# S5 phase tables: computed in a preparation thread and kept in DRAM, or computed inside each S5 pair

## The chip, the cores and the metric

The kernel runs on one core of one Trainium2 chip. The metric is the device time of one execution in microseconds (us). The kernel before takes 1314.66 us (median of three runs: 1306.43, 1314.66 and 1315.25 us). "Faster" and "slower" are meant against that median.

## The reference

The reference is a trunk of four mixers, each followed by `x = layer_norm(ALPHA * x + mixer(x))`: gated linear attention (GLA), gated delta net (GDN), a state-space layer (S5), and GLA again. It is run twice: on one prompt of 512 tokens from a zero state, and on 8 samples of 8 tokens from given states. The model has 1024 channels; everything is float32, and all new states are outputs.

The S5 layer matters here. Its input projection gives `u` and a gate `z`, each 1024 wide. Its 64 groups have 16 channels and a complex diagonal state of 64 entries, with `h[t] = a * h[t-1] + B u[t]` and `y[t] = Re(C h[t]) + D u[t]`. Then come gelu, a gated linear unit with two 1024 x 1024 weights (`s5_glu`), the gate, and an output projection. The decay `a` is a magnitude times a phase. The kernel works on blocks of 8 tokens, so a prompt has 64 blocks, and it needs for every block index n the phase `a8^n` (cosine and sine) and the magnitude `r8`.

## The kernel before

**Tiling.** Channels lie on the 128 partitions, tokens along the free dimension (2 halves of 256 prompt and 32 sample tokens, 288 columns). Every dense projection is split into a rounded and a remainder part for activations and weights, and is written as three passes of `fp32r` matmuls with 288 moving columns. These are the matmuls `ps<-fx`. Weights come from DRAM through three raw buffers, and are split by ScalarE and VectorE into a ring of four slots. The matmuls of the recurrences themselves are float32 (`ps<-sb`).

**Order of the work.** The program is written as generator threads, each with a rank (a lower rank goes first), over the recording engine queues of the class `Core`. A planner, run when the program is built, keeps a model clock. Whenever an engine is free in that model, the ready operation of the lowest rank is put next on that engine's queue. On the chip each engine and the SP queue, which issues all DMAs, then works its queue strictly in that written order. All records pass through one helper, so every instruction bears line 408. The dense projections (rank 10) run through all layers as one stream; recurrence threads fill the queues beside them.

**Memory.** Scratch memory is one pool of 32,960 words per partition. A thread gets a piece only when the pool holds that piece and the words that its thread must leave free (`keep`), and otherwise waits for a free. The dense stream leaves `reserve` words (2500 during GDN). GDN pairs after the first leave 2000. S5 pair j leaves 3500 until all earlier pairs have signalled `h`:

```
            if sum(h[1] for h in self.holes) >= prod(shape) + keep():
                v = self.alloc(shape, dt, long)
...
                self.go(self.s5_pair(g, j), 3 + j, f's5_{j}',
                        lambda j=j: 0 if all(f'h{i}' in self.events for i in range(j)) else 3500)
```

**The S5 preparation** is the thread `s5_prep0` (line 1899, rank 3), which starts with the kernel and runs beside GLA and GDN. It computes the angles of 6 doublings (`lc`, `ls`, 6 x 32 words each) and the magnitude `r8` (32 words), then calls `s5_prep` four times (tables stored to DRAM as `s5G`, `s5C`, `s5K`), then `s5_phase` four times. One `s5_phase` (line 2037) takes a table `R` of 3 x 8 x 64 words and two scratch pieces of 256 words. GpSimd sets three columns, VectorE copies `r8` into a plane of 8 x 63, and six doublings of six VectorE operations each (over 8, 16, 32, 64, 128 and 256 elements) fill the cosine and sine planes. The table is then stored to DRAM (`s5R`, 768 KB). Last, eight transfers rearrange `s5K` into `s5Kx` (512 KB each), and `s5prep` is signalled.

**The S5 pairs** (`s5_pair`, line 2217, ranks 3 to 6). There are four, with 16 groups each. Pair j starts once the constants are there (`s5c`) and, for j > 1, once `u` of unit 2j-1 is stored. It loads half a table (`st <- s5G`) and its phase table (`R <- s5R`), and waits for `u` of units 2j and 2j+1. It allocates and loads `U` (1,152 words, eight transfers from `Ud`), allocates `E` (1,024 words) and `Es`, and multiplies. Then VectorE rotates by `R`, scans and rotates back. The starting states come into `H` by a transfer of 64 KB from `s5_h1`. Four VectorE operations complete `H`, and `h{j}` is signalled. Two products with `s5Kx` and `s5C`, a gelu, eight stores to `Yd` and one load give `yx{2j}` and `yx{2j+1}`, which the dense stream waits for, one after the other, in its first three `s5_glu` units (`fm_first`, 18 matmuls for each `yx`).

Of the kernel before, what the change touches and what calls it, by code (L numbers as in the profile page):

```python
# [19 lines left out]
P = 128  # L20
# [3 lines left out]
NS, LS = 8, 8  # L24
# [7 lines left out]
S5_G, S5_P, S5_C, S5_T, S5_N = 64, 64, 16, 8, 72  # L32
# [582 lines left out]
class Kernel(Core):  # L615
# [779 lines left out]
    def gdn_gates(self, g, pab):  # L1395

        yield from self.wait('gdnpre')
        R = (yield from self.A(640))[:40]
        self.gpsimd.memset(R, 0.0)
        t1, t2 = (yield from self.A(2, HW)), (yield from self.A(2, HW))  # L1400
# [18 lines left out]
        for src, p0 in ((u2, 0), (ab[32:40], 32)):  # L1419
            d = R[p0:p0 + 8]  # L1420
            self.cp(d[:, 0:512].rearrange("p (a n) -> p a n", a=2), src[:, :, 0:256])
            for i in range(2):
                self.cp(d[:, 512 + 64 * i:576 + 64 * i].rearrange("p (a n) -> p a n", a=2), src[:, :, 256:HW])
        self.free(pab, t1, t2)
        yield R
        self.sync.dma_start(out=g['gcd'], in_=R[0:8, 0:576])
        self.sig('gcd')
        pc = yield from self.bank()
        for c in range(5):
            self.tensor.transpose(pc[:, c * 40:c * 40 + 40], R[:, c * P:c * P + P], self.ident[:40, :40])  # L1430
        C = yield from self.A(5, 40)
# [467 lines left out]
    def s5_prep0(self):  # L1899
# [3 lines left out]
        s = self.s5v = {}  # L1903
        tmp = []

        def T(name, *shape):
            s[name] = t = yield from self.A(*(shape or (G,)), long=True)
            if not shape:
                tmp.append(t)
            return t  # L1910
# [18 lines left out]
        lc, ls, r8 = (yield from T('lc', 6, 32)), (yield from T('ls', 6, 32)), (yield from T('r8', 32))  # L1929
# [53 lines left out]
        self.Kx = self.dram('s5Kx', [P, S5_G, P])  # L1983
        self.Gd = self.dram('s5G', [8, P, 8, P])
        self.Cd = self.dram('s5C', [8, P, 8, P])
        self.Rd = self.dram('s5R', [4, P, 3, 8, 64])
        z = yield from self.A(8, P)
        self.gpsimd.memset(z, 0.0)
        yield z
# [4 lines left out]
        for j in range(4):  # L1994
            yield from self.s5_prep(j)
        self.free(*[s[n] for n in ('sgn', 'ar', 'ai', 'cre', 'cim', 'ars', 'ais', 'dT', 'delta')])
        for j in range(4):
            yield from self.s5_phase(j)
        self.free(s['lc'], s['ls'], s['r8'])
        for t in range(S5_T):  # L2000
            self.sync.dma_start(out=self.Kx[16 * t:16 * t + 16], in_=self.Kd[:, :, 16 + 16 * t:144 + 16 * t]
                                .rearrange("g c n -> c g n"))
# [34 lines left out]
    def s5_phase(self, j):  # L2037

        s, t2 = self.s5v, self.TT
        q = slice(8 * j, 8 * j + 8)  # L2040
        R = yield from self.A(3, 8, 64)
        m1, m2 = (yield from self.A(8, 32)), (yield from self.A(8, 32))
        self.gpsimd.memset(R[:, 0, :, 0:1], 1.0)
        self.gpsimd.memset(R[:, 1, :, 0:1], 0.0)
        self.gpsimd.memset(R[:, 2, :, 0:1], 0.0)
        self.vector.tensor_copy(out=R[:, 2, :, 1:], in_=s['r8'][:, q].unsqueeze(2).to_broadcast([P, 8, 63]))
        for k in range(6):
            n = 1 << k
            cb, sb = (v.unsqueeze(2).to_broadcast([P, 8, n]) for v in (s['lc'][:, k, q], s['ls'][:, k, q]))
            rc, rs = R[:, 0, :, 0:n], R[:, 1, :, 0:n]  # L2050
            a, b = m1[:, :, 0:n], m2[:, :, 0:n]
            t2(a, rc, cb, ALU.mult)
            t2(b, rs, sb, ALU.mult)
            t2(R[:, 0, :, n:2 * n], a, b, ALU.subtract)
            t2(a, rc, sb, ALU.mult)
            t2(b, rs, cb, ALU.mult)
            t2(R[:, 1, :, n:2 * n], a, b, ALU.add)
            yield R[:, 1]
        self.free(m1, m2)
        yield R  # L2060
        self.sync.dma_start(out=self.Rd[j], in_=R)
        self.free(R)

    def s5_prep(self, b):

# [106 lines left out]

    def s5_consts(self, g):
        yield from self.wait('s5prep')
        g['h2'] = self.load((yield from self.A(3, 32, NS, long=True)), 's5_h2')
        g['bg'] = self.load((yield from self.A(16, long=True)), 's5_bglu')
        g['hs'] = yield from self.A(2, 32, NS, long=True)
        g['hp'] = yield from self.A(S5_G, long=True)
        self.sig('s5c')
# [37 lines left out]
    def s5_pair(self, g, j):  # L2217

        N, NP = S5_N, S5_N - NS
        def maps(src):  # L2220
            st = yield from self.A(8, P)
            self.load(st, None, src)
            return st

        yield from self.wait('s5c', *([f'u{2 * j - 1}'] if j > 1 else []))
        st = yield from maps(self.Gd[2 * j])
        R = yield from self.A(3, 8, 64)
        self.load(R, None, self.Rd[j])
        yield from self.wait(f'u{2 * j}', f'u{2 * j + 1}')
        U = yield from self.A(16, N)  # L2230
        for s in range(S5_T):
            self.sync.dma_start(out=U[16 * s:16 * s + 16],
                                in_=g['Ud'][j][:, :, :, s].rearrange("m g c n -> c (m g) n"))
# [36 lines left out]
        self.TT(M2, E[:, ::-1], sb, ALU.mult)  # L2270

        H = yield from self.A(16, N + 1)
        self.load(H[:, :, 0:NS], None, self.a['s5_h1'][:, 16 * j:16 * j + 16])
        self.gpsimd.memset(H[:, :, NS:NS + 1], 0.0)
        yield [M1, M2]
        for ri in range(2):
# [8 lines left out]
        hs, t = g['hs'][:, :, q], (yield from self.A(2, 8, NS))  # L2285
# [28 lines left out]
        if j == 3:  # L2314
            yield [g['hs'], g['hp']]
            self.sync.dma_start(out=self.o['s5s'], in_=g['hs'])
            self.sync.dma_start(out=self.o['s5p'], in_=g['hp'])
            self.free(g['hs'], g['hp'], g['h2'])
        yield from self.wait('udead')
        yield yf  # L2320
        for e in range(2):
# [58 lines left out]
```

## Time and profile before

| | |
|---|---|
| runs | 1306.43, 1314.66, 1315.25 us |
| profiled execution | 1305.55 us, of which the span is 1303.7 us |
| instructions | 23,541 |
| busy | TensorE 96%, VectorE 74%, ScalarE 46%, GpSimd 13% |
| DMA | 198.35 MB moved, mean 152 GB/s |
| granted TensorE clock, mean | 0.986 of 2.4 GHz |

Rough stretches of the profile, in us from the span's start: first GLA to about 255, its output projection to 312, GDN to about 640, its output projection to 713, S5 input projections to 875, gated unit and output projection to about 1000, last GLA to the end. The preparation thread stores its phase tables between 277.5 and 386.8 us, and writes `s5Kx` from 386.1 to 406.5 us.

How to read it: a busy TensorE says little by itself, since ends of matmuls are modelled; the matmul count in a stretch and the granted clock say how fast it went. Waits name the work that ended last before an instruction could start. "SPq" is the queue that issues the DMAs.

### The profile page before, as it was taken

The page shows a single profiled execution, that of the slowest core. Times are in us where ns is not written, and L with a number is a line of the kernel's source. Part 1 is how long each engine was busy: PE and PEld are TensorE (multiplying, and loading weights), DVE is VectorE, ACT ScalarE, POOL GpSimd, SP SyncE. Part 2 cuts the span into 40 slices and gives each one's busy share as a digit, 9 for nine tenths or more (in the row PEclk, how much of TensorE's full clock was granted, in tenths as well). Part 3 has the DMA queues.
Part 4 walks back from the last instruction along what each step waited for, and adds up shares of the span by engine and source line. Part 5 has one row for each costly group of instructions (what it writes and reads, how often), then busy time and mean ns, then how long its engine had stood idle before and what let it go on. Part 6 is the DMA issues. An engine that isn't in the chain of part 4 may idle for free.

```text
span 1303.7 us, 23541 instructions
## 1 busy us (share of the span) xinstructions
PE 1255.2 (96%) x8795; PEld 1175.5 (90%) x8795; DVE 964.5 (74%) x2117; ACT 599.9 (46%) x1317; POOL 164.6 (13%) x303
## 2 busy tenths in 40 slices
PE   9999999999998899999999999999999999999997
PEld 8898998779998888999987999999998899999986
DVE  5989888999998989989679439544245877554557
ACT  5565454514966667555442334453232255343330
POOL 5510000011221311232002000000000200000001
PEclk9999999999998999999999989999999999999999
DMA  7335645734368727445364798862234423243242
GB/s 230 115 97 163 208 138 165 252 103 166 102 167 241 183 80 201 122 134 158 118 223 168 217 246 195 231 194 89 81 115 152 141 96 115 88 140 128 98 154 73
DMA packets 129537, 198.35 MB, mean 152 GB/s; under 512 B 47176, under 2 KB 85960, under 8 KB 127376
## 3 DMA queue, kind: packets, MB, share of 16 engines
q1 hardware_dynamic: 129424, 196.86, 49.8%
q8 instruction: 69, 1.13, 0.4%
q14 instruction: 44, 0.36, 0.1%
HBM read 153.64 MB, written 47.37 MB: 154 GB/s over the span
## 4 chain that ended last, share of the span: by engine, by line
PE 62%; DVE 22%; DMA 6%; ACT 4%; issue 4%; POOL 1%; SPq 1%; POOLq 0%; DVEq 0%; ACTq 0%
PE ps L408 62%; DVE sb L408 18%; DVE fx L408 4%; ACT sb L408 3%; DMA sb<-Ud 2%; POOL sb L408 1%; ACT L408 1%; ACT fx L408 1%; SPq L408 1%; DMA s5Kx<-s5K 1%; DMA sb<-in_gdn_s 0%; DMA sb<-scr 0%; DMA sb<-in_rst 0%; DMA sb<-s5Kx 0%; DMA sb<-in_gla_q 0%
## 5 line engine op out<-in xcount | busy, mean ns | idle before, releaser
L408 PE MATMUL ps<-fx 128*128 128x288 f32 (+2 forms) x6736 | 1045.0, 312 | 8.0 <-ACT sb L408 2.9
L408 PEld LDWEIGHTS ps<-fx 128*128 128x128 f32 x6736 | 947.8, 190 | 57.6 <-issue 6.5
L408 DVE TENSOR_TENSOR fx<-sb,fx 128x1024 fp32r<-128x1024 f32 (+5 forms) x308 | 252.8, 845 | 164.5 <-ACT fx L408 160.8
L408 ACT CAST fx<-sb 128x1024 fp32r<-128x1024 f32 (+5 forms) x312 | 221.1, 735 | 302.1 <-PE ps L408 257.4
L408 PE MATMUL ps<-sb 128*128 128x128 f32 (+10 forms) x2059 | 292.7, 292 | 32.3 <-DVE sb L408 17.7
L408 PEld LDWEIGHTS ps<-sb 128*128 128x128 f32 (+6 forms) x2059 | 244.3, 175 | 61.9 <-DVE sb L408 20.4
L408 DVE TENSOR_TENSOR sb<-sb 128x128 f32<-128x128 f32 (+26 forms) x667 | 263.9, 414 | 13.5 <-ACT sb L408 3.9
L408 ACT COPY sb<-ps 128x512 f32<-128x512 f32 (+10 forms) x233 | 91.8, 411 | 120.6 <-PE ps L408 66.0
L408 ACT ACTIVATE sb<-sb 128x128 f32<-128x128 f32 (+10 forms) x239 | 108.9, 504 | 72.7 <-DVE sb L408 63.6
L408 DVE SCALAR_TENSOR_TENSOR sb<-sb 128x512 f32<-128x512 f32 (+7 forms) x205 | 133.5, 660 | 10.2 <-POOL sb L408 7.4
L408 POOL TENSOR_TENSOR sb<-sb 128x1 f32<-128x1 f32 (+4 forms) x46 | 72.5, 1581 | 526.6 <-DVE sb L408 511.0
L408 DVE SCALAR_TENSOR_TENSOR sb<-sb,ps 128x256 f32<-128x256 f32 (+3 forms) x216 | 92.1, 457 | 38.1 <-PE ps L408 27.5
L408 ACT ACTIVATE sb<-ps 128x128 f32<-128x128 f32 (+2 forms) x176 | 66.9, 382 | 74.7 <-DVE sb L408 40.4
L408 DVE SCALAR_TENSOR_TENSOR sb<-ps,sb 128x128 f32<-128x128 f32 (+3 forms) x112 | 55.2, 502 | 31.8 <-PE ps L408 25.3
L408 DVE COPY sb<-ps 128x256 f32<-128x256 f32 (+8 forms) x99 | 37.8, 388 | 51.0 <-PE ps L408 32.5
L408 POOL COPY sb<-sb 128x24 f32<-128x24 f32 (+4 forms) x92 | 40.2, 460 | 237.6 <-DVE sb L408 138.5
L408 ACT CAST fx<-ps 128x512 fp32r<-128x512 f32 (+2 forms) x32 | 17.6, 550 | 74.5 <-PE ps L408 74.4
L408 ACT ACT_TABLE_LOAD x37 | 47.5, 1283 | 1.3 <-PEq L2369 0.7
L408 ACT ACTIVATE sb<-ps,sb 128x128 f32<-128x128 f32 (+2 forms) x93 | 37.9, 440 | 21.1 <-PE ps L408 18.4
L408 POOL MEMSET sb<- 128x3 f32 (+10 forms) x96 | 29.3, 328 | 125.7 <-DVE sb L408 55.9
L408 POOL CAST fx<-sb 128x32 fp32r<-128x32 f32 (+1 forms) x33 | 10.6, 351 | 227.2 <-PE ps L408 199.8
L408 ACT ACTIVATION_READ_ACCUMULATOR sb<-ps 128x1 f32 x136 | 27.2, 200 | 0.1
(25 smaller groups left out, 250.4 us busy)
## 6 DMA issues: line engine op xcount, KB each, us to landing
sb<-in_gla_v SPq DMA_DIRECT2D x16, 512.0 KB, 3.7
sb<-in_gla_r SPq DMA_DIRECT2D x16, 512.0 KB, 4.0
sb<-in_gla_s SPq DMA_DIRECT2D x8, 1024.0 KB, 6.2
out_s_gla<-sb SPq DMA_DIRECT2D x8, 1024.0 KB, 4.3
sb<-in_gla_out SPq DMA_DIRECT2D x16, 512.0 KB, 3.7
sb<-in_gdn_s SPq DMA_DIRECT2D x32, 256.0 KB, 3.4
sb<-in_s_glu SPq DMA_DIRECT2D x16, 512.0 KB, 4.3
xres<-sb SPq DMA_DIRECT2D x12, 512.0 KB, 3.2
```

What stands on the lines that cost most here:

```text
L408: fn(*args, **kw)
```

## The change

The phase table is no longer computed in the preparation thread and stored. Each S5 pair calls `s5_phase` in place of its load of `R`, and uses the table that it returns. The angles `lc`, `ls` and `r8` (416 words) are freed after the fourth call instead of at the end of the preparation. The starting states `s5_h1` are loaded once, whole (512 words, 256 KB), with the S5 constants, and each pair's `H` is filled by a GpSimd copy from them instead of by a transfer.

```
--- before.py
+++ after.py
@@ -1983,7 +1983,6 @@
         self.Kx = self.dram('s5Kx', [P, S5_G, P])
         self.Gd = self.dram('s5G', [8, P, 8, P])
         self.Cd = self.dram('s5C', [8, P, 8, P])
-        self.Rd = self.dram('s5R', [4, P, 3, 8, 64])
         z = yield from self.A(8, P)
         self.gpsimd.memset(z, 0.0)
         yield z
@@ -1994,9 +1993,6 @@
         for j in range(4):
             yield from self.s5_prep(j)
         self.free(*[s[n] for n in ('sgn', 'ar', 'ai', 'cre', 'cim', 'ars', 'ais', 'dT', 'delta')])
-        for j in range(4):
-            yield from self.s5_phase(j)
-        self.free(s['lc'], s['ls'], s['r8'])
         for t in range(S5_T):
             self.sync.dma_start(out=self.Kx[16 * t:16 * t + 16], in_=self.Kd[:, :, 16 + 16 * t:144 + 16 * t]
                                 .rearrange("g c n -> c g n"))
@@ -2057,9 +2053,10 @@
             t2(R[:, 1, :, n:2 * n], a, b, ALU.add)
             yield R[:, 1]
         self.free(m1, m2)
-        yield R
-        self.sync.dma_start(out=self.Rd[j], in_=R)
-        self.free(R)
+        s['phases'] = s.get('phases', 0) + 1
+        if s['phases'] == 4:
+            self.free(s['lc'], s['ls'], s['r8'])
+        return R
 
     def s5_prep(self, b):
 
@@ -2172,6 +2169,7 @@
 
     def s5_consts(self, g):
         yield from self.wait('s5prep')
+        g['h1'] = self.load((yield from self.A(S5_G, NS, long=True)), 's5_h1')
         g['h2'] = self.load((yield from self.A(3, 32, NS, long=True)), 's5_h2')
@@ -2224,8 +2222,7 @@
 
         yield from self.wait('s5c', *([f'u{2 * j - 1}'] if j > 1 else []))
         st = yield from maps(self.Gd[2 * j])
-        R = yield from self.A(3, 8, 64)
-        self.load(R, None, self.Rd[j])
+        R = yield from self.s5_phase(j)
         yield from self.wait(f'u{2 * j}', f'u{2 * j + 1}')
@@ -2270,7 +2267,7 @@
         H = yield from self.A(16, N + 1)
-        self.load(H[:, :, 0:NS], None, self.a['s5_h1'][:, 16 * j:16 * j + 16])
+        self.gpsimd.tensor_copy(out=H[:, :, 0:NS], in_=g['h1'][:, 16 * j:16 * j + 16])
         self.gpsimd.memset(H[:, :, NS:NS + 1], 0.0)
@@ -2315,7 +2312,7 @@
-            self.free(g['hs'], g['hp'], g['h2'])
+            self.free(g['hs'], g['hp'], g['h1'], g['h2'])
```

## Rows read from the trace of the kernel before

**Rows 1.** The page's part 1: busy us, share of the span, instructions.
```profile
PE 1255.2 (96%) x8795; PEld 1175.5 (90%) x8795; DVE 964.5 (74%) x2117; ACT 599.9 (46%) x1317; POOL 164.6 (13%) x303
```
**Rows 2.** Windows: length, busy us (instructions) of PE, PEld, DVE, ACT, POOL; clock, DMA share, GB/s.
```profile
350.00:390.00 40.00, 38.41 (x279) 37.51 (x279) 38.02 (x111) 29.78 (x74) 10.44 (x29) 1.00 0.57 154
...
710.00:730.00 20.00, 15.89 (x113) 14.55 (x113) 14.31 (x25) 5.09 (x8) 0.62 (x2) 1.00 0.82 303
730.00:750.00 20.00, 20.00 (x152) 20.00 (x151) 6.24 (x7) 7.49 (x9) 0.00 (x0) 1.00 0.67 166
```
**Rows 3.** Windows, as above, of two short disturbed stretches and one in GDN.
```profile
395.00:400.00 5.00, 2.84 (x22) 2.60 (x20) 4.93 (x13) 2.85 (x11) 0.21 (x1) 0.98 1.07 318
400.00:410.00 10.00, 7.85 (x25) 6.59 (x26) 8.27 (x31) 6.84 (x31) 0.32 (x1) 0.50 1.04 305
765.00:770.00 5.00, 3.12 (x21) 2.92 (x19) 1.23 (x1) 1.14 (x2) 0.00 (x0) 0.84 1.03 332
770.00:780.00 10.00, 10.00 (x50) 10.00 (x50) 5.16 (x12) 3.38 (x9) 0.00 (x0) 0.57 0.95 251
450.00:460.00 10.00, 6.96 (x38) 6.23 (x39) 8.96 (x27) 9.94 (x23) 0.66 (x2) 0.83 0.59 160
```
**Rows 4.** Timeline of DVE, the second phase table: start, us, instructions merged, count.
```profile
310.98 1.97 DVE L408 TENSOR_TENSOR sb<-sb 128x16 f32<-128x16 f32 x11
...
313.47 5.09 DVE L408 TENSOR_TENSOR sb<-sb 128x64 f32<-128x64 f32 x16
```
**Rows 5.** DVE groups by form, 257.5 to 386.5 us: busy us, mean ns, idle before.
```profile
L408 DVE TENSOR_TENSOR sb<-sb 128x16 f32<-128x16 f32 x24 | 3.6, 174 | 0.3
...
L408 DVE COPY sb<-sb 128x504 f32<-128x504 f32 x4 | 1.7, 416 | 1.6 <-DMA s5R<-sb 1.6
```
**Rows 6.** The chain of waits, 311 to 414 us: start, us, what.
```profile
318.59 3.37 DMA s5R<-sb
...
406.46 6.93 DMA s5Kx<-s5K
```
**Rows 7.** Timeline of PE: start, us, what, count, idle before and its releaser.
```profile
401.57 2.07 PE L408 MATMUL ps<-sb 128*128 128x256 f32 x4 [3.73 <-DVE sb L408]
...
768.08 6.79 PE L408 MATMUL ps<-sb 128*128 128x72 f32 x32 [1.88 <-issue]
...
836.87 19.71 PE L408 MATMUL ps<-fx 128*128 128x288 f32 x146
```
**Rows 8.** Timeline of the SP queue: start, us of issuing, transfer, count.
```profile
393.58 1.75 SPq L408 DMA_DIRECT2D sb<-in_gdn_q  x1
...
747.31 0.43 SPq L408 DMA_DIRECT2D sb<-s5R  x1
...
761.22 0.44 SPq L408 DMA_DIRECT2D sb<-Ud  x1
...
799.82 1.80 SPq L408 DMA_DIRECT2D sb<-Ud  x4
...
815.81 5.19 SPq L408 DMA_DIRECT2D Yd<-sb  x8
...
822.07 0.39 SPq L408 DMA_DIRECT2D sb<-s5G  x1
```
**Rows 9.** The page's part 6, DMA issues: count, KB each, median us to landing.
```profile
sb<-Ud SPq DMA_DIRECT2D x32, 72.0 KB, 6.3
```
**Rows 10.** Timeline of DVE and ACT at the end of the S5 pairs.
```profile
846.59 1.39 DVE L408 TENSOR_TENSOR sb<-sb 64x512 f32<-64x512 f32 x2 [1.40 <-DMA sb<-in_s_h]
...
882.64 2.72 DVE L408 TENSOR_TENSOR fx<-sb,fx 128x512 fp32r<-128x512 f32 x4
...
876.00 0.65 ACT L408 ACTIVATE sb<-ps 128x576 f32<-128x576 f32 x1
```
**Rows 11.** Timeline of POOL: two copies of one shape in GDN.
```profile
332.29 0.21 POOL L408 COPY sb<-sb 128x24 f32<-128x24 f32 x1
...
336.56 1.17 POOL L408 COPY sb<-sb 128x24 f32<-128x24 f32 x1
```

More of the change, by code (lines that the diff above doesn't have):

```diff
@@ L1985, in s5_prep0 @@
         self.Cd = self.dram('s5C', [8, P, 8, P])
-        self.Rd = self.dram('s5R', [4, P, 3, 8, 64])
         z = yield from self.A(8, P)
@@ L1996, in s5_prep0 @@
         self.free(*[s[n] for n in ('sgn', 'ar', 'ai', 'cre', 'cim', 'ars', 'ais', 'dT', 'delta')])
-        for j in range(4):
-            yield from self.s5_phase(j)
-        self.free(s['lc'], s['ls'], s['r8'])
         for t in range(S5_T):
@@ L2059, in s5_phase @@
         self.free(m1, m2)
-        yield R
-        self.sync.dma_start(out=self.Rd[j], in_=R)
-        self.free(R)
+        s['phases'] = s.get('phases', 0) + 1
+        if s['phases'] == 4:
+            self.free(s['lc'], s['ls'], s['r8'])
+        return R
     def s5_prep(self, b):
@@ L2174, in s5_consts @@
         yield from self.wait('s5prep')
+        g['h1'] = self.load((yield from self.A(S5_G, NS, long=True)), 's5_h1')
         g['h2'] = self.load((yield from self.A(3, 32, NS, long=True)), 's5_h2')
@@ L2226, in s5_pair @@
         st = yield from maps(self.Gd[2 * j])
-        R = yield from self.A(3, 8, 64)
-        self.load(R, None, self.Rd[j])
+        R = yield from self.s5_phase(j)
         yield from self.wait(f'u{2 * j}', f'u{2 * j + 1}')
@@ L2272, in s5_pair @@
         H = yield from self.A(16, N + 1)
-        self.load(H[:, :, 0:NS], None, self.a['s5_h1'][:, 16 * j:16 * j + 16])
+        self.gpsimd.tensor_copy(out=H[:, :, 0:NS], in_=g['h1'][:, 16 * j:16 * j + 16])
         self.gpsimd.memset(H[:, :, NS:NS + 1], 0.0)
@@ L2317, in s5_pair @@
             self.sync.dma_start(out=self.o['s5p'], in_=g['hp'])
-            self.free(g['hs'], g['hp'], g['h2'])
+            self.free(g['hs'], g['hp'], g['h1'], g['h2'])
         yield from self.wait('udead')
```

## The prediction

> **What bounds the kernel now.** I read the shares of busy time first [rows 1]: TensorE is busy 96% of the span, the next engine, VectorE, 74%. So at most some 48 us of TensorE's idle time can be won, plus what it loses where it is busy at a low clock. The windows come next, because that loss has places. In the stretch where the second half of the phase tables is computed, TensorE is idle 1.6 of 40 us while VectorE is busy 38.0 [rows 2]: VectorE is full there, but TensorE hardly waits for it. Two short places are much worse [rows 3]. From 395 to 410 us TensorE is idle 2.16 + 2.15 = 4.3 us, and for the last 10 us its granted clock is 0.50, the lower of its levels of 1.2 and 2.4 GHz; the 7.85 us in which it was busy there did half their work, 3.9 us lost. Together 8.2 us. From 765 to 780 us it is idle 1.88 us, and loses 3.12 x 0.16 + 10.00 x 0.43 = 4.8 us at granted clocks of 0.84 and 0.57. Together 6.7 us. In both places the DMA share is 0.95 to 1.07: all sixteen engines are in use. In both the low clock follows a wait of TensorE [rows 7].
>
> The queue and the chain say what filled the DMA engines. At the first place it is the eight `s5Kx` copies, which begin when the last phase table is done; one of them stands with 6.93 us in the chain of waits, and an earlier phase-table store with 3.37 us [rows 6]. A GDN weight is issued among them at 393.58 [rows 8], and TensorE stops soon after. At the second place the load of pair 2's table (768 KB, issued 747.31) goes ahead of most of pair 1's `U` transfers, the last of which is issued at 761.22 [rows 8]; with the usual 6.3 us to landing [rows 9] that gives 767.5, and TensorE's wait ends at 768.08 [rows 7]. The profile names no releaser there, so this is a reading.
>
> **The change part by part.**
>
> *The tables leave the preparation.* One table is 37 VectorE operations: 1.97 + 5.09 us for 27 of them [rows 4], one copy of 0.42 us and nine of the smallest at about 0.17 us [rows 5], together 9.0 us; four are 36 us. They go from a stretch where VectorE is full. What that frees goes to the GDN threads and to weight splits; on TensorE it is worth no more than its idle time there, 1.6 us, and I count it as nothing, with gains of up to 1.6 us. Four stores of 768 KB go too, with the GpSimd instructions that queue behind one.
>
> *The `s5Kx` copies move* ahead of where the tables were, from 386 to 406 us to right behind the last `s5_prep`, by about 285 us. The weights in flight there are those of GDN's first units, which run only from about 312 us, so I expect no new wait; they also no longer meet GDN's solve. That should take away most of the 8.2 us. But GDN's next hard stretch is short of memory rather than of DMA: from 450 to 460 us TensorE is idle 3.0 us [rows 3], and the dense stream, which must leave 2500 words, stands still there by the sizes of the code until GDN's pieces are freed. It now also lacks the 416 words of the angles. Between a full gain of 8.2 us and a loss as large as one more such stretch (3.0 us and 6.96 x 0.17 = 1.2 us at the low clock, 4.2 us) I take a gain of 6 us, nearer to the measured stall, since its cause is gone.
>
> *The tables enter the pairs.* Pairs 0 and 1 start both at about 710 us, while VectorE still finishes the layer norm; from 710 to 750 us it is idle 5.7 + 13.8 = 19.5 us [rows 2], which holds the 18 us of two tables, and their `U` is loaded only at 742 us and later. Layer-norm operations have lower ranks, but each may wait behind a table operation of up to 0.42 us: 1 us lost, between 0 and the 4.1 us that TensorE idles there today. Pair 2's table has the time from 747 us to its `u`. The load of its `R` is gone from the front of pair 1's `U` loads; of the 6.7 us I take 3, because the `U` transfers still share the engines with weights (bounds 0 and 6.7).
>
> *Pair 3 and memory.* This is where the change adds a wait. By the sizes of the code, pair 3 asks for `U` (1,152 words) with 3,500 to be left, 4,652 in all; when pair 1 signals `h1` it finds 4,944 and loads from 799.82 us [rows 8]. With 512 words of `s5_h1` more in use it finds 4,432, and must wait until pair 0 is done, whose `Yd` stores begin at 815.81 [rows 8]. `E` had to wait for that moment before, too, so the first product, then possible at about 816, now waits for eight issues of 0.45 and a landing of 6.3 us [rows 8, 9], and perhaps for the 5.2 us of the `Yd` issues ahead: 10 to 15 us. Part of that was lost anyway, since the second half's table was issued only at 822.07 [rows 8]: with 6 us of it back, 4 to 9 us. The 1.4 us that VectorE waited for `s5_h1` in pair 3 goes [rows 10]. Against this stands slack: the last `z` unit is done by 876.0, six `yx` parts of 18 matmuls at 19.71/146 = 0.135 us take 14.6 us more, so pair 3's result is needed by 890.6 at the latest, and its last write ends at 885.4 [rows 7, 10]: 5.2 us. 4 to 9 less 1.4 less 5.2 is a stall of 0 to 2.4 us; I take 2 us lost.
>
> *`s5_h1` in one transfer, copied by GpSimd.* Four transfers of 64 KB become one of 256 KB, early. The copies have 128 elements; the nearest rows are GpSimd copies of 24, which took 0.21 us, or 1.17 us while VectorE worked on two inputs [rows 11]. The place is beside two such VectorE operations, so up to 1.2 us each, under operations that `H` waits for anyway: nothing, bounds 0 and 1 us for each of four.
>
> The Trainium skill, "SBUF — State Buffer", section "Who interferes with whom", speaks against this step: a VectorE instruction with two inputs in SBUF and a GpSimd instruction that reads SBUF exclude one another, so that the later one waits for the whole of the earlier. The two copies bear it out (0.21 against 1.17 us). By the rule alone each new copy would cost an operation's length, some 5 us for four; by the rows it falls beside the same two operations.
>
> The sum is -6 + 1 - 3 + 2 = -6 us. The profiled execution (1305.55 us: the span of 1303.7 and 1.85 around it) would come to 1299.5. It lies 9.1 us under the median of the three runs, of which one is near it and two are near 1315; I put the same difference to the median: **1308 us**.
>
> **The rivals.**
>
> *Both bad places go whole, and the next ones too.* For it: each has one named transfer as its neighbour, and the change removes or moves exactly these. Against: 36 us of VectorE work remain. 8.2 + 6.7 + 1.6 = 16.5 us off: 1298 us.
>
> *The gain is given back.* TensorE is 96% busy, its queue order is written against a model, and GDN waits for memory in any case. If the dense stream, ahead by 6 us, stands still that much longer at 450 us, the first gain is gone; with S5's 3 us against 1 and 2 the time is 1314 us, up to 1322 with the extra stretch of 4.2 us and the upper bound of layer norm.
>
> *Slower: pair 3 late.* One mechanism: `U` refused for 220 words. It decides from the point where pair 3's last write falls after 890.6 us. With the whole 15 us and none back, TensorE stands 15 - 5.2 = 9.8 us, and such a wait is followed by a low clock, 4.8 us as measured at 765. With the other terms absent: 1314.7 + 14.6 = 1329 us. Against: six of the 15 us were lost before, too.
>
> *The tables are not hidden in the pairs.* If a pair's 9 us stood between its `u` and its `U`, pair 3 would end 9 us later. The code puts the table before the wait for `u`, and pair 3 begins when `u5` is stored, two units before `u7`: no separate case, but part of the slower one.
>
> **How the numbers follow.** I take about 1%, 13 us, for what a measurement of this kernel can tell from no change: its own runs lie 9 us apart. Chances: forecast 0.45 (1302 to 1313), both places whole 0.21, given back 0.21, pair 3 late 0.13. Faster by over 1% is under 1301.5: the second case and 0.03 of the first, 0.24. Slower by over 1% is above 1327.8: 0.12 of the last case and 0.01 of the third, 0.13. The rest, 0.63, is within 1%. The range 1291 to 1324 leaves out 0.06 below and the last case above.
>
> **What would show it.** Right: no `s5R` transfer; `s5Kx` issued before 300 us; granted clock 1.00 and no wait of several us near 400 us; `U` of pair 1 landed before TensorE comes to it, with no low clock near 770; `U` of pair 3 issued only after pair 0's `Yd` stores; TensorE going on without a wait through the first gated units. Wrong: a wait before the last `yx` parts with a low clock behind it, VectorE late at the layer norm (waits of TensorE near 715 us above 4.1 us), or a longer standstill of dense matmuls in GDN. The forecast falls first if the written order of GDN changes so far that new waits arise where none is now; no row can price that.

## The result and the profile after

The changed kernel takes **1318.72 us** (median of 10 runs, 1315.05 to 1323.52), the kernel before, on the same chip, 1311.05 us (median of 10, 1304.83 to 1315.25): a ratio of **1.0069**, 95% interval 1.0044 to 1.0093. That is a loss of some 8 us where a gain of 6 was forecast; it lies inside the range, and within the 1% that were taken for no change. The two profiled executions differ by 11.0 us: the span is 1314.7 us instead of 1303.7.

Part 1 of the page of the changed kernel, as in [rows 1]:

```profile
span 1314.7 us, 23536 instructions
...
PE 1253.8 (95%) x8795; PEld 1175.3 (89%) x8795; DVE 962.5 (73%) x2109; ACT 591.3 (45%) x1316; POOL 169.1 (13%) x307
```

VectorE, ScalarE and TensorE do nearly the same work; the 11 us are time in which TensorE stands or runs at its lower clock. To see where, I add up, over windows of 5 us, TensorE's idle time (length less busy) and what its clock cost (busy times 1 less the granted clock). The three stretches are GDN, the S5 pairs with the units around them, and the first gated units (us lost, of one profiled execution each):

| kernel | span | 340 to 700 | 700 to 860 | 860 to 920 |
|---|---|---|---|---|
| before | 1303.7 | 25.4 | 12.3 | 0.0 |
| after | 1314.7 | 24.2 | 13.3 | 11.1 |

The loss is at the end of the S5 pairs. In the kernel before, TensorE is busy without a break there (columns as in [rows 2]):

```profile
880.00:900.00 20.00, 20.00 (x152) 20.00 (x152) 11.88 (x16) 9.15 (x12) 0.00 (x0) 1.00 0.22 67
```

The windows there and at the places of [rows 2, 3], of the changed kernel (columns as there):

```profile
350.00:390.00 40.00, 34.78 (x239) 33.62 (x238) 30.62 (x73) 21.83 (x62) 7.31 (x24) 0.96 0.47 124
395.00:400.00 5.00, 5.00 (x40) 4.51 (x39) 4.94 (x13) 4.51 (x9) 1.24 (x3) 1.00 0.10 10
402.60:405.60 3.00, 0.03 (x2) 0.02 (x1) 2.97 (x9) 2.74 (x8) 0.00 (x0) 0.98 0.72 192
400.00:410.00 10.00, 6.21 (x28) 4.89 (x26) 9.69 (x36) 5.79 (x25) 0.00 (x0) 0.83 0.65 184
760.00:765.00 5.00, 5.00 (x26) 5.00 (x25) 1.76 (x10) 1.46 (x5) 0.00 (x0) 0.50 1.02 370
765.00:770.00 5.00, 5.00 (x31) 5.00 (x31) 4.44 (x21) 1.28 (x4) 0.00 (x0) 0.77 0.96 233
770.00:780.00 10.00, 9.50 (x77) 9.26 (x75) 8.36 (x16) 5.21 (x15) 0.00 (x0) 1.00 0.61 117
710.00:730.00 20.00, 19.88 (x150) 19.29 (x149) 19.58 (x68) 6.99 (x10) 1.77 (x9) 1.00 0.60 220
...
450.00:460.00 10.00, 9.90 (x78) 9.48 (x77) 9.25 (x32) 7.11 (x23) 0.20 (x1) 1.00 0.37 91
880.00:900.00 20.00, 11.79 (x82) 11.27 (x81) 3.06 (x5) 2.19 (x4) 0.00 (x0) 0.84 0.29 70
```

From 880 to 900 us TensorE is idle 8.2 us and its clock is down to 0.84. The first of these stretches, 350 to 390, got worse although VectorE has 7.4 us less to do there: TensorE is idle 5.2 us instead of 1.6. The timeline of TensorE of the changed kernel shows what it waits for in GDN:

```profile
358.72 2.00 PE L408 MATMUL ps<-sb 128*128 128x256 f32 x8 [1.39 <-DVE sb L408]
364.54 2.77 PE L408 MATMUL ps<-fx 128*128 128x288 f32 x10 [3.83 <-DVE sb L408]
...
405.58 3.61 PE L408 MATMUL ps<-sb 128*128 128x256 f32 x8 [2.97 <-ACT sb L408]
410.60 1.59 PE L408 MATMUL ps<-fx 128*128 128x288 f32 x10 [1.42 <-DVE sb L408]
```

The `s5Kx` copies are long over (issued from 261.99 us on), and the wait of 3.73 us of [rows 7] is there again, some 4 us later, as 2.97 and 1.42, with ScalarE and VectorE as releasers. From 395 to 400 us, where the copies had filled the DMA engines, the share is 0.10 and TensorE is busy throughout; during the wait itself, 402.60 to 405.60, it is 0.72 from other loads, while VectorE is busy 2.97 and ScalarE 2.74 of the 3.00 us. In S5 the wait for `U` moved as well, from pair 1 to the first product of all:

```profile
758.31 7.08 PE L408 MATMUL ps<-sb 128*128 128x72 f32 x32 [3.72 <-DMA sb<-Ud]
...
780.46 1.98 PE L408 MATMUL ps<-sb 128*128 128x72 f32 x16 [0.96 <-DMA sb<-Ud]
```

Pair 3's loads, in SP's queue of the changed kernel (against 799.82 for `U` and 822.07 for the second half's `s5G` in [rows 8]):

```profile
810.23 0.33 SPq L408 DMA_DIRECT2D sb<-Ud  x1
...
811.57 1.11 SPq L408 DMA_DIRECT2D sb<-Ud  x2
812.78 5.89 SPq L408 DMA_DIRECT2D Yd<-sb  x8
...
819.70 2.10 SPq L408 DMA_DIRECT2D sb<-Ud  x4
...
823.12 7.50 SPq L408 DMA_DIRECT2D Yd<-sb  x8
830.67 0.44 SPq L408 DMA_DIRECT2D sb<-Ud  x1
...
837.76 0.32 SPq L408 DMA_DIRECT2D sb<-s5G  x1
```

Five of the eight `U` transfers are issued behind `Yd` stores; the last one is out at 831.1 us, against 806.7 in the kernel before. What follows on TensorE, and on VectorE the last write of pair 3's result:

```profile
835.83 1.90 PE L408 MATMUL ps<-sb 128*128 128x72 f32 x16
...
884.99 3.71 PE L408 MATMUL ps<-fx 128*128 128x288 f32 x26
896.28 0.58 PE L408 MATMUL ps<-fx 128*128 128x288 f32 x1 [7.57 <-DVE fx L408]
897.49 7.67 PE L408 MATMUL ps<-fx 128*128 128x288 f32 x46 [0.63 <-DVE fx L408]
```
```profile
895.51 0.62 DVE L408 CAST fx<-sb 128x512 fp32r<-128x512 f32 x1 [21.26 <-issue]
896.17 2.44 DVE L408 TENSOR_TENSOR fx<-sb,fx 128x512 fp32r<-128x512 f32 x4
```

TensorE has run out of other work at 888.7 (the end of the matmuls that start at 884.99) and stands 7.57 + 0.63 us. The last write ends at 898.6; it ended at 885.4 before, so it is 13.2 us later, of which the slack of 5.2 took its part.

### The profile page after: what moved, and what is told of

Its sections match the earlier page's. It is cut to its first block, busy times and chain, and to the rows that moved or that the text cites. A ratio compares the mean times of both kernels' runs of the same rounds, so it can differ in the third digit from the quotient of the medians.

```text
span 1314.7 us, 23536 instructions
## 1 busy us (share of the span) xinstructions
PE 1253.8 (95%) x8795; PEld 1175.3 (89%) x8795; DVE 962.5 (73%) x2109; ACT 591.3 (45%) x1316; POOL 169.1 (13%) x307
## 5 line engine op out<-in xcount | busy, mean ns | idle before, releaser
L408 PE MATMUL ps<-fx 128*128 128x288 f32 (+2 forms) x6736 | 1048.0, 312 | 21.3 <-DVE fx L408 9.6
L408 ACT CAST fx<-sb 128x1024 fp32r<-128x1024 f32 (+5 forms) x316 | 224.2, 736 | 291.6 <-PE ps L408 244.1
L408 DVE TENSOR_TENSOR sb<-sb 128x128 f32<-128x128 f32 (+34 forms) x667 | 264.9, 416 | 15.9 <-ACT sb L408 5.9
L408 ACT ACTIVATE sb<-sb 128x128 f32<-128x128 f32 (+8 forms) x244 | 109.4, 501 | 78.2 <-DVE sb L408 71.1
L408 DVE SCALAR_TENSOR_TENSOR sb<-sb 128x600 f32<-128x600 f32 (+7 forms) x205 | 133.1, 662 | 14.9 <-POOL sb L408 8.0
L408 POOL COPY sb<-sb 128x24 f32<-128x24 f32 (+4 forms) x96 | 44.8, 486 | 268.3 <-DVE sb L408 162.6
L408 DVE COPY sb<-ps 128x256 f32<-128x256 f32 (+7 forms) x95 | 36.3, 388 | 55.0 <-PE ps L408 33.6
L408 DVE CAST fx<-sb 32x256 fp32r<-32x256 f32 (+3 forms) x26 | 9.7, 372 | 25.0 <-issue 21.3
```

Of the source, the lines that this page charges most:

```text
L408: fn(*args, **kw)
```

## The experiments

Ratios are to the kernel before, run on the same chip beside them. Four ideas were to be told apart. **M**: pair 3's `U` is refused for want of memory. **H**: only the 512 words of `s5_h1` matter. **V**: the tables' VectorE work in the pairs costs. **N**: any shift makes the planner write another order, and the order is what costs. Other letters are explained in the expectations that use them.

**Memory alone.** The kernel before, with words held and never used:

```diff
+ g['unused'] = yield from self.A(288, long=True)   # e6_hold304: 304
```

> The kernel before, with a piece of 288 words held, and never used, from the S5 constants to the end of pair 3; nothing else is changed. Theory M (pair 3's U is refused because the pool is a few words short, so its loads wait for pair 0 to finish, and TensorE waits for yx6): by the sizes pair 3 finds 4,656 words and needs 4,652, so U is loaded as before; ratio to the kernel before 0.998 to 1.002, no wait of TensorE in the first gated units. Rival V (the tables' 36 us of VectorE work inside the pairs make the after-kernel late): no table is moved here, so 0.998 to 1.002 too. Rival N (any change of the written order costs half a per cent by chance): anything from 0.994 to 1.008.

> The same with 304 words: 16 words more, which nobody uses. Theory M: pair 3 finds 4,640 words where it needs 4,652; its U is issued only when pair 0 is done, some 10 us or more later than before (799.8 us), and TensorE waits 4 to 9 us before the parts yx6 and yx7, with a low clock behind it; 8 to 13 us slower than the kernel before, ratio 1.006 to 1.010. Rival V: 0.998 to 1.002, as with 288 words. Rival N: 0.994 to 1.008, with no fixed place of the loss.

Measured: 288 words 1307.26 us, ratio 0.9983 (0.9951 to 1.0014); 304 words 1320.83 us, ratio 1.0092 (1.0060 to 1.0123). Sixteen unused words per partition cost 13.6 us between the medians. TensorE before the gated units, first with 288, then with 304 words:

```profile
871.00 34.24 PE L408 MATMUL ps<-fx 128*128 128x288 f32 x255
```
```profile
900.12 0.58 PE L408 MATMUL ps<-fx 128*128 128x288 f32 x1 [4.37 <-DVE fx L408]
901.33 3.94 PE L408 MATMUL ps<-fx 128*128 128x288 f32 x15 [0.63 <-DVE fx L408]
```

255 matmuls without a wait, to the end of the view, against the wait of the changed kernel. M is shown: `U` needs 4,652 words free and the kernel before has 4,944, so that 292 may go and 304 may not. The two programs are written in the same order up to this request; from there on `U` is out by 803.9 us with 288 words and by 823.8 with 304. The traces show 7.3 us at the place of the wait. Over all their runs the mean granted clock is 0.985 with 288 and 0.978 with 304; times some 1,255 us of busy TensorE that is 9 of the 13.6 us (an estimate), of which the trace has 2.3 us behind the wait. Where the rest of the lower clock lies is open.

**The refusal taken out of the change**, and `s5_h1` taken out of it:

```diff
- ... else 3500)
+ ... else 3200 if j == 3 else 3500)                      # e3_keep
```
```diff
- g['h1'] = self.load(..., 's5_h1'); self.gpsimd.tensor_copy(out=H[...], in_=g['h1'][...])
+ self.load(H[:, :, 0:NS], None, self.a['s5_h1'][...])     # e1_h1_dma, in each pair
```

> The kernel after, with one number changed: pair 3 must leave 3,200 words instead of 3,500 until the earlier pairs are through. Its U then needs 4,352 words and finds 4,432. All table work stays in the pairs, and s5_h1 stays in the pool. Theory M: U is issued near 800 us, the wait of 8 us before yx6 is gone, 8 to 13 us faster than the kernel after, so 0.996 to 1.001 of the kernel before. Rival V: the VectorE work is unchanged, so the time stays at 1.005 to 1.009 of the kernel before.

> The kernel after without its second half: s5_h1 comes by one transfer per pair again, and nothing of it is held; the tables stay in the pairs. Rival H (the 512 words of s5_h1 alone are what refuses U): U is in time, 0.996 to 1.001 of the kernel before. Theory M in its wider form (the pool is short by hundreds of words at that moment, and who is refused depends on which of pairs 1, 2 and 3 asks first; with the tables in the pairs, pair 2 asks for its 2,048 words of products before pair 3 gets U): U is late all the same, 1.004 to 1.009. Rival V: 1.005 to 1.009.

Measured: e3 1314.87 us, ratio 1.0036 (1.0010 to 1.0062), by the medians half of the loss (the interval meets that of the changed kernel) and outside what was expected; e1 1324.93 us, ratio 1.0112 (1.0061 to 1.0163), slower still. H falls: without the 512 words, by the planner's counts, pair 2 takes the 2,048 words of its products ahead of `U`, which goes out from 815 to 833 us, and TensorE waits 7.57 us before 906. In e3 the wait before the gated units is gone (208 matmuls in a row to the end of the view), and something else has come; TensorE's timeline, then the windows:

```profile
809.50 13.04 PE L408 MATMUL ps<-sb 128*128 128x72 f32 x60 [2.85 <-DMA sb<-s5C]
...
877.25 27.97 PE L408 MATMUL ps<-fx 128*128 128x288 f32 x208
```
```profile
810.00:820.00 10.00, 10.00 (x49) 10.00 (x48) 7.28 (x10) 1.94 (x3) 0.00 (x0) 0.50 0.98 268
820.00:830.00 10.00, 10.00 (x47) 10.00 (x46) 3.03 (x5) 2.44 (x9) 0.99 (x5) 0.50 0.40 67
```

An `s5C` map is 2.85 us late, and behind this wait TensorE works 20 us at a granted clock of 0.50: 10 us of work lost. From 700 to 860 this execution loses 25.1 us instead of the changed kernel's 13.3; that took back what `U` had given (11.1 less 1.1 from 860 to 920).

**Each part by itself**, without a refusal (pair 3 at 3,200 words in all four):

```diff
  # e9_keep_only: the kernel before with 3,200 words, nothing else
  # e7_kx_keep: and the s5Kx copies ahead of the phase tables
  # e8_h1_keep: e9 and s5_h1 loaded once, copied by GpSimd
  # e10_late_kx: the changed kernel, with
+ yield self.now + 110.0
  for t in range(S5_T):
      self.sync.dma_start(out=self.Kx[...], ...)
```

> The kernel before, with pair 3 asked to leave 3,200 words instead of 3,500 when it takes U. By the planner's counts U then goes out once u7 is there, ahead of h1. Pair 3 had 5.2 us of slack in the kernel before, so all theories expect the same time within 0.3% (ratio 0.997 to 1.003). It is what the three other runs are compared with: it shows what the lower limit alone does, apart from any part of the change.

> The kernel before with the s5Kx copies ahead of the phase tables and pair 3 at 3,200 words; tables still stored and read, s5_h1 in four transfers. It is the Kx part of the change alone, with no refusal of U. Theory K (the moved copies put GDN into a worse order, and that is the rest of the loss that the run with 3,200 words kept): ratio 1.002 to 1.005, with TensorE losing more between 340 and 480 us than the 17.3 us of before. Theory V (the tables in the pairs are the rest): 0.993 to 0.999, with the low clock near 400 us gone. The prediction's term was -6 us: 0.995.

> The kernel before with s5_h1 loaded once and copied by GpSimd, and pair 3 at 3,200 words, so that U goes out when pair 1 signals h1, as in the kernel before. It is the s5_h1 part of the change alone with no refusal of U. Theories K and V: no change, ratio 0.997 to 1.003, the four copies being hidden and the wait for s5_h1 in pair 3 (1.4 us of VectorE) gone. Theory C (the GpSimd copies hold VectorE's chain in each pair, and that is the rest of the loss): 1.002 to 1.005, with waits of VectorE for GpSimd in the pairs.

> The changed kernel with pair 3 at 3,200 words, and the s5Kx copies put off by 110 us of the planner's time, to about where they stood before the change; the tables stay in the pairs. It gives the Kx part of the change back. Theory K: the ratio falls from 1.0036 to 0.998 to 1.001, although the low clock near 400 us may return. Theory V: it stays at 1.003 or rises to 1.008, since the stall near 400 us returns (the prediction's 6 us) and the S5 pairs are as late as with the change. U goes out just ahead of h1 by the planner's counts.

Measured: e9 0.999 (0.997 to 1.001), e7 1.0025 (1.0001 to 1.0049), e8 0.9977 (0.9953 to 1.0001), **e10 0.9932** (0.9905 to 0.9959; 1303.11 us, the fastest of all). The `s5_h1` part costs nothing that shows. With the copies early the kernel before is some 4 us slower (e7 against e9), and with them moved back the changed one is faster than both kernels. V falls as the reason for the loss, since e10 has all four tables in the pairs; what they cost by themselves is not shown. In e10 the lower limit plays no part: its order is the same with 3,500, since by the planner's counts `U` is taken ahead of `h1` with 7,264 words free. So late copies alone cure the refusal, too. This looked like theory K, but the places didn't fit: e7 loses 30.7 us from 340 to 700 (e9 22.7), whereas e10 and e3 hardly differ there (22.9 and 24.4) and differ by 14 us from 700 to 860 (10.9 and 25.1). And e7's trace makes up from 700 to 860 for what it loses in GDN (10.4 against e9's 21.3). These are single executions, e10's the fastest of its runs and e3's near the slowest; but the clock parts the two in every run, 0.986 to 0.990 in e10 against 0.977 to 0.983 in e3.

**Place or order.** The same with other delays, and one run that halves the `s5C` loads (each pair takes its first map for both halves):

```diff
+ yield self.now + 60.0        # e14_kx60; 30.0: e19_kx30; 120.0: e18_kx120
```
```diff
- sc = yield from maps(self.Cd[m])
+ sc = sc if e else (yield from maps(self.Cd[m]))     # e15_half_c
```

> The changed kernel with pair 3 at 3,200 words and the s5Kx copies put off by 60 us of the planner's time instead of 110. Measured so far: no delay 1.0036, 110 us 0.9932. Theory P (what costs is where the copies stand, between the last s5_prep and GDN's first units): they now stand beside GDN's first units, near 310 to 330 us, and the ratio lies between the two, 0.996 to 1.000. Theory N (the copies' place matters only because every shift of them makes the planner write another order for everything behind; each order meets S5's full DMA engines with other waits): anything from 0.993 to 1.005, read from the S5 stretch (700 to 920 us) and not from GDN's: the runs with 30, 60 and 120 us need not lie in a line.

> The same with a delay of 30 us. Theory P: 1.000 to 1.003, nearer to no delay. Theory N: anything from 0.993 to 1.005, with the loss between 340 and 700 us within 3 us of the other delays' and the difference in the S5 stretch.

> The same with a delay of 120 us, 10 more than in the fastest so far. Theory P: no change from the 110 us run, 0.992 to 0.995. Theory N: it may as well be 5 to 10 us slower (up to 1.002), by waits in the S5 stretch that the 110 us run does not have. By the planner's counts its U for pair 3 is taken 6 us behind h1.

> The changed kernel with pair 3 at 3,200 words and no delay of the copies; each pair uses its first s5C map (512 KB) for both halves, so the second half's products are computed from the wrong map and four loads of 512 KB are left out. It bears on what gave U's gain back in the run with 3,200 words: there TensorE waited 2.85 us for an s5C map at 809 us and ran at a granted clock of 0.50 for the 15 us behind it. Theory D (the maps of the y products come late because the DMA engines are full, and the wait with its low clock is what is lost): that wait and the low clock from 805 to 830 us go, and the ratio falls from 1.0036 by 6 to 12 us, to 0.994 to 0.999. Rival (GDN's worse order is the rest of the loss): below 3 us of change, 1.001 to 1.004.

Measured: 30 us 1.0020 (0.9995 to 1.0045), 60 us 1.0014 (0.9984 to 1.0045), 120 us **1.0064** (1.0041 to 1.0088), half of `s5C` 1.0027 (1.0003 to 1.0052). Ten microseconds of delay, 110 to 120, take the ratio from 0.9932 to 1.0064. P expected no change there and falls; N stands. Only its expectation of where was wrong: the windows of e10, then of e18, show the loss in GDN.

```profile
340.00:480.00 140.00, 128.10 (x927) 122.13 (x925) 119.99 (x345) 87.90 (x248) 26.81 (x74) 0.96 0.56 150
480.00:700.00 220.00, 215.19 (x1532) 198.93 (x1532) 184.05 (x495) 118.50 (x339) 37.40 (x75) 0.99 0.53 152
```
```profile
340.00:480.00 140.00, 123.86 (x879) 117.61 (x878) 114.32 (x309) 80.15 (x220) 23.37 (x64) 0.94 0.54 146
480.00:700.00 220.00, 209.58 (x1509) 195.03 (x1508) 180.89 (x508) 120.91 (x355) 34.10 (x74) 0.98 0.51 149
```

With no work changed, TensorE is busy 9.9 us less in these 360 us, before the lower clock is counted. The copies' own traffic isn't beside it: e18's last copy is issued at 403.42 us, and by the same sums its extra loss lies from 440 to 460 us (11.6 against 2.6) and from 520 to 540 us (7.4 against 0.0). Its longest wait there is for ScalarE:

```profile
444.25 5.19 PE L408 MATMUL ps<-sb 128*128 128x96 f32 x25 [4.89 <-ACT sb L408]
```

The run with half of `s5C` doesn't bear out D: its median, 1314.25 us, is that of e3 (1314.87), although four loads of 512 KB are gone. Its profiled execution was its fastest run, 1306.42 us, and that of e3 near its slowest, 1317.49. The two traces have nearly the same wait at the same place, and only e3's has the low clock behind it. TensorE and the windows of the run with half of `s5C`:

```profile
808.44 6.78 PE L408 MATMUL ps<-sb 128*128 128x72 f32 x59 [2.27 <-DMA sb<-s5C]
```
```profile
810.00:820.00 10.00, 10.00 (x87) 10.00 (x87) 9.88 (x13) 4.53 (x13) 0.46 (x3) 1.00 0.66 160
820.00:830.00 10.00, 9.65 (x83) 9.44 (x81) 1.97 (x4) 4.71 (x5) 0.60 (x3) 1.00 0.97 286
```

**Is the kernel before as sensitive?** Its copies put off by 10 and 20 us, and the changed kernel's by 100:

```diff
+ yield self.now + 10.0        # e20_before_10 (limit 3,200); 20.0: e21_before_20
+ yield self.now + 100.0       # e22_kx100: the changed kernel, limit 3,200
```

> The kernel before (with pair 3 at 3,200 words, measured 0.999), with the s5Kx copies put off by 10 us of the planner's time and nothing else: no instruction is added or left out. Theory N (any shift of the copies makes the planner write another order, and an order is worth up to about 1%): the ratio leaves 0.996 to 1.002 as easily as not; 0.995 to 1.010, with the loss in GDN (340 to 700 us) changed by up to 10 us, as between the changed kernel's delays of 110 and 120 us. Theory S (the order of the kernel before is robust, and only the change's own parts make it sensitive): 0.997 to 1.002.

> The same with 20 us. Theory N: 0.995 to 1.010, and not between the runs with 0 and 10 us. Theory S: 0.997 to 1.002.

> The changed kernel with pair 3 at 3,200 words and the copies put off by 100 us, between the runs with 60 us (1.0014) and 110 us (0.9932). By the planner's counts pair 3's U is refused again until 12 us after h1. Theory N with theory M (U late): slower than both neighbours, 1.003 to 1.012. Theory P (the copies' place alone): between its neighbours, 0.993 to 1.001.

Measured: **1.0065** (1.0041 to 1.0088), **0.9952** (0.9933 to 0.9971) and 1.0209 (1.0182 to 1.0237). S falls. The kernel before, with nothing added or left out, moves by 17 us between 10 and 20 us of delay, more than the change moved it. Two waits of e20 in GDN, behind its last copy (416.77 us); from 425 to 455 us e9 waits 1.23 us at most:

```profile
445.37 0.71 PE L408 MATMUL ps<-sb 128*128 128x128 f32 x4 [2.09 <-ACT sb L408]
449.94 5.11 PE L408 MATMUL ps<-sb 128*128 128x128 f32 x22 [3.85 <-issue]
```

And e22, in which `U` is refused again until 12 us after `h1`, has both losses at once, more than expected:

```profile
917.66 0.58 PE L408 MATMUL ps<-fx 128*128 128x288 f32 x1 [4.60 <-DVE fx L408]
```

The same sums as in the first table, for the experiments:

| kernel | span | 340 to 700 | 700 to 860 | 860 to 920 |
|---|---|---|---|---|
| before, 288 words held | 1311.8 | 22.2 | 22.9 | 0.0 |
| before, 304 words held | 1319.0 | 23.3 | 21.9 | 7.3 |
| before, 3,200 (e9) | 1311.1 | 22.7 | 21.3 | 0.0 |
| e9, copies 10 us later | 1320.6 | 33.5 | 17.3 | 3.8 |
| e9, copies 20 us later | 1302.9 | 27.2 | 10.0 | 0.0 |
| after, 3,200 (e3) | 1315.6 | 24.4 | 25.1 | 1.1 |
| e3, copies 60 us later | 1307.2 | 29.8 | 8.9 | 0.0 |
| e3, 100 us | 1337.1 | 34.9 | 22.4 | 11.4 |
| e3, 110 us (e10) | 1298.8 | 22.9 | 10.9 | 0.0 |
| e3, 120 us | 1312.0 | 35.2 | 11.7 | 0.0 |

## Why the prediction was wrong

By its own stretches the sum was -6 in GDN, -3 + 1 in the layer norm and S5, +2 before the gated units. The two profiles give -1.2, +1.0 and +11.1.

- **The step that failed by its size: pair 3, "with 6 us of it back ... I take 2 us lost".** The mechanism was foreseen to the word count, the point of 890.6 us nearly so (TensorE ran dry at 888.7), and it was priced at 2 us in the sum and given 0.13 as a rival. The slack was right: the last write came 13.2 us later, and 13.2 - 5.2 = 8.0 us is about the stand of 7.57 + 0.63. Wrong was the delay of 4 to 9 us. Nothing came back: the second half's `s5G` was put off with the rest, by 15.7 us (837.76 against 822.07), and the `U` transfers stood in SP's queue among two pairs' `Yd` stores (5.89 and 7.50 us of issuing), while the working had allowed for one. With the low clock after the wait the term is +11. The rival's 9.8 us of standing was near; of its 4.8 us for the clock 1.7 came.
- **The step that failed in its mechanism: the `s5Kx` move, "since its cause is gone", -6.** The copies did go, the DMA share from 395 to 400 us fell from 1.07 to 0.10, and TensorE still waits in GDN's first units, 2.97 and 1.42 us some 4 us later, for ScalarE and VectorE. VectorE had been named as the releaser of the 3.73 us in [rows 7]; I had gone by the transfers that ran beside it. A neighbour in time isn't a cause: by its releasers the stall is GDN's own chain, in VectorE and ScalarE. Other loads still run beside it (share 0.72), so the copies are cleared as its cause, and DMA traffic as such is not. That the copies by themselves bring no gain is what e7 shows, in the one order that it has.
- **The tables out of the preparation, nothing:** VectorE is busy 30.6 instead of 38.0 us from 350 to 390, and TensorE idles more. Freed VectorE time brought a different order, not a gain. From 450 to 460 the feared standstill didn't come: busy 9.90 at a clock of 1.00.
- **Layer norm, +1 lost: a gain instead.** From 710 to 730 TensorE is busy 19.88 us instead of 15.89, beside 19.58 us of VectorE work: the tables fit under it, and 4.0 us of idle time went.
- **Pair 1's `U`, -3: turned into another wait.** The load of `R` is gone, and the first product of pairs 0 and 1 waits 3.72 us for `Ud`, with a clock of 0.50 from 760 to 765 and 0.77 to 770. By the sums of the tables, 750 to 780 us loses 8.4 us instead of 7.1. The rest of S5, 780 to 860 us, which had no term of its own, loses 4.6 instead of 1.1.
- **`s5_h1`, nothing: right.** Its wait in [rows 10] is gone, and e8 measures no loss. The group of the four new GpSimd copies, busy us and mean ns:

```profile
L408 POOL COPY sb<-sb 128x128 f32<-128x128 f32 x4 | 2.3, 569 | 3.7 <-DMA Yd<-sb 3.7
```

A mean of 0.57 us lies between the two ends of [rows 11]. Three of the four took 0.30 to 0.37 us; the fourth, at 800 us, stood beside a VectorE operation with two inputs of 1.23 us and took 1.30. The Trainium skill, "SBUF — State Buffer", section "Who interferes with whom", has such a copy, where it comes second, wait for the whole of a VectorE instruction with two inputs; the trace agrees in the fourth. The prediction's 5 us by that rule had all four beside such an operation. They took 2.3 us in all, and nothing waited for them.

The forecast's last sentence named what would fell it first, a written order so changed that new waits arise, and gave it no price. It has one now. Whether the whole change is a gain or a loss is not a property of its three edits: with the copies 110 us later the same edits give 0.9932, 10 us further on (pair 3 at 3,200 words) 1.0064. What is shown of the loss as it was measured: refused memory is worth 13.6 us on the kernel before; on the changed kernel, with that gone, about half of the loss is left by the medians, and it goes or stays with the order. **Open** is what makes one order good: I found the place of the loss in each trace, in GDN or in S5, and no quantity that tells it beforehand. Open, too, is what the tables in the pairs are worth by themselves, because they can't be moved without writing a new order.

## What to carry to other kernels

Where a planner writes the order, first measure what a shift that changes no work does (put off one transfer by 10 and by 20 us): an effect below that spread, here over 1%, can't be read off a trace, nor be credited to the edit, unless two programs keep the same order up to the place, as with 288 and 304 words. Count the memory of each request against what is free at the moment it is made; a request that passes by 292 words is a cliff, and 304 unused words went over it. Put a stall down to the releaser that the trace names before the traffic beside it: here the named traffic was moved away, and the stall stayed.

## What the runs showed of the hardware

After a short wait among the products of 72 columns, TensorE's granted clock can go to 0.50, 1.2 GHz, and stay there while TensorE is busy 10.00 of 10 us, as in e3 from 810 to 830 us, where that costs 10 us of work; from 830 to 835 us, TensorE still busy 5.00 of 5, it was back at 1.00. It doesn't follow from the wait's length alone: behind the 1.88 us of [rows 7] the clock was 0.57 from 770 to 780 us [rows 3], and behind 2.27 us in e15 it stayed at 1.00.

The runs of a single kernel spread by about as much, 1302.31 to 1316.03 us in 35 runs of the kernel before, and the mean granted clock of each run goes with it: the seven of these runs at 0.987 and 0.988 took 1305.0 us in the mean, the five at 0.977 to 0.979 1314.9. A clock lower by 0.0095 over some 1,255 us of busy TensorE is 12 us (an estimate), so the clock can account for the spread. With one trace of each kernel it is not shown in which stretch it falls.
